# Modulation sums of ten of twelve blocks on ScalarE and GpSimd inside the attention loop, and a gated branch sum on VectorE instead of GpSimd

## The chip, the cores and the metric

The kernel runs on one core of a Trainium2 chip. The metric is the time of one execution on the device in microseconds (us), as the median of repeated runs. A profile of one execution is used beside it.

## What is computed

One layer of a hybrid backbone over 1024 latent tokens and 128 context tokens, with 1024 channels in float32. Of the reference this matters here:

```python
def modulation(cvec, w_ada, b_ada):
    m = jax.nn.silu(cvec) @ w_ada + b_ada
    return [t[:, None, :] for t in jnp.split(m, 6, axis=-1)]

def merge_branches(u_f, attn_o, g, w_fo, w_ao, w_out):
    gates = jax.nn.sigmoid(g)
    g_f, g_a = gates[..., :D_MODEL], gates[..., D_MODEL:]
    m = g_f * (fourier_mix(u_f) @ w_fo) + g_a * (attn_o @ w_ao)
    return m @ w_out
```

The layer is: modulated RMSNorm, one input projection that gives a Fourier branch, queries, keys and values (16 heads, 4 key heads, banded over blocks of 128 tokens) and two gate vectors; then the merge above, the output projection with a gated residual, and a squared-ReLU MLP with a gated residual. The modulation is two matrix-vector products (the conditioning vector and the context vector, called tokens 0 and 1) with a 1024 x 6144 matrix, w_ada. Its six parts are needed at different times: shift and scale of the first norm at once, the other four parts only from the output projection on.

## The kernel before, in words

All matrix products are done as three products of split operands: a float32 operand is cast to a reduced type ("hi", on ScalarE), the rest is taken by a subtraction ("lo", mostly on VectorE, helper `sub`, L138), and TensorE multiplies hi by hi, hi by lo and lo by hi (`mm3`, L191 to L193). Tokens lie in nine tiles of 128.

The program runs in stages. First the input is normalised and modulated, and the Fourier columns are projected. Then four Fourier groups are transformed (the loop over `gi`): per group a first product, an eviction to `pqh`/`pql` (L543 on ScalarE and L138 on VectorE), and a second product. Between them stand "filler" units, gate projections that TensorE can do at any time (`filler`; 48 units of 24 matmuls). Then keys and values are projected (`evac_kv`, with the rotary embedding `apply_rope`). Then comes attention: 36 units (4 key groups x 9 query tiles). The loop over units emits for unit s the queries of unit s+1, the scores of unit s (`attention_scores`, two pairs of heads), and the output of unit s-1 (`attention_out`). In `attention_scores` a pair of heads goes matmul (L691, L692), masked maximum (VectorE, L693), exponential (ScalarE, L705), reciprocal (VectorE, L713) and normalisation (GpSimd, L715). In `attention_out` the weights are transposed (TensorE, L729), split (ScalarE L734, VectorE L138) and multiplied with the values (L739, L740). Then come the Fourier output projections (`f_unit`), the attention output projection with the merge (8 column blocks x 3 token chunks, 24 turns, L905 to L914), the output projection, and the MLP.

The modulation of the four late parts is cut into 16 blocks of 256 columns, each block into ten steps (`mod_blocks`). Steps 0 to 7 load a 128 x 256 piece of w_ada (`mraw`, L296) and add its product with the two tokens to an accumulator `macc` (VectorE, L300 for the first piece, L302 for the others; two instructions per step). Steps 8 and 9 transpose and reduce the accumulator (VectorE, L311, L312). `mod_fold` (called at step 5 of the following block) sums over partitions by a matmul (TensorE, L265) and adds the bias (L269). `mod_step(n)` emits the next n steps. The constants place them: 30 steps (three blocks) in the Fourier loop (`MOD_F`), one step after each of units 1 to 30 (`MOD_A`), three steps in each merge turn (`MOD_2`) until 40 are left (`MOD_LATE`: 60 steps, six blocks), and the last four blocks in the MLP.

The order of instructions on an engine is not that of the text: a scheduler places each engine's instructions by its own model of times, `tc.issue_after(x)` keeps work from being placed before x, and from then on each engine and each queue works strictly in its order. SP issues almost all DMAs, in order too. The MLP's first piece is ordered by hand and is the same in both kernels.

```python
                for e in range(2):
                    nc.gpsimd.tensor_scalar(pt[:, e, :n], pt[:, e, :n], mx[:, 6 + e : 7 + e], 1.0, ALU.mult, ALU.mult)
                pts.append(pt)
...
                nc.vector.tensor_tensor(zf, zf, zp, ALU.mult)
                nc.gpsimd.tensor_tensor(z, z, zf, ALU.add)
```

## Time and profile before

| | |
|---|---|
| median of 3 runs | 1741.18 us (1739.69 to 1743.17) |
| the profiled execution | 1740.25 us |
| its span, first to last instruction | 1738.5 us |
| TensorE busy in the span | 1660.2 us, 95% |
| VectorE, ScalarE, GpSimd busy | 1217.1 us (70%), 846.3 us (49%), 229.2 us (13%) |
| mean granted TensorE clock | 0.982 |

In the profile PE is TensorE's matmuls, PEld its weight loads, DVE VectorE, ACT ScalarE, POOL GpSimd, and SP the queue that issues DMAs. Busy shares are averages over stages; the clock column is the granted clock as a part of full speed (1.2 GHz stands as 0.50, 2.4 GHz as 1.00).

### The profile page before, as it was taken

Reading aid. Unit: us, or ns where it says so; the run is one execution under the profiler, and the core shown is the slowest. Engines: PE = TensorE matmul, PEld = TensorE weight load, DVE = VectorE, ACT = ScalarE, POOL = GpSimd, SP = SyncE. Lnnn points to the kernel's source line nnn. Section 1 sums busy time; section 2 is a strip of 40 time slices with the busy share of each in tenths; the row PEclk is TensorE's granted clock in tenths of the full one; section 3 lists DMA queues with packets and bytes.
Section 4 is the critical chain, followed back from the end, with each engine's and each line's share of the span. In section 5 each row is a group of like instructions: output and inputs, shape, how many; then the busy total and the mean of one; then the engine's idle time right before and its main releaser. Section 6 shows DMA issues by size and latency. Waiting matters only on the chain.

```text
span 1738.5 us, 26472 instructions
## 1 busy us (share of the span) xinstructions
PE 1660.2 (95%) x9101; PEld 1480.9 (85%) x9101; DVE 1217.1 (70%) x2538; ACT 846.3 (49%) x1676; POOL 229.2 (13%) x310
## 2 busy tenths in 40 slices
PE   6999988999999999999899889999999999999998
PEld 5788878999899999999888688888888788888886
DVE  7595455686767777659968878767666488777764
ACT  7443134555646556655326663444444345444542
POOL 3410002212213222202211400000000100000000
PEclk9999999999999999999999989999999999999999
DMA  9462383032222211478655435444444997566751
GB/s 293 124 189 82 129 233 76 28 96 68 60 53 63 59 35 40 147 241 281 211 165 204 160 103 176 164 146 164 151 146 155 231 378 252 190 193 193 238 176 61
DMA packets 218759, 267.44 MB, mean 154 GB/s; under 512 B 30768, under 2 KB 150144, under 8 KB 218624
## 3 DMA queue, kind: packets, MB, share of 16 engines
q1 hardware_dynamic: 210368, 255.79, 46.3%
q0 software_dynamic: 8256, 9.96, 2.2%
q8 instruction: 72, 1.18, 0.3%
q14 instruction: 63, 0.52, 0.1%
HBM read 196.20 MB, written 69.48 MB: 153 GB/s over the span
## 4 chain that ended last, share of the span: by engine, by line
PE 43%; DVE 4%; DMA 2%; ACT 1%; issue 1%; POOL 0%; SPq 0%; ACTq 0%; DVEq 0%; POOLq 0%
PE x L1570 6%; PE x L1569 6%; PE x L1568 6%; PE x L1179 5%; PE x L1181 5%; PE x L1180 5%; PE x L1015 1%; PE x L1016 1%; PE x L1017 1%; DVE macc L302 1%; PE mm L1570 1%; PE mm L1569 1%; PE mm L1568 1%; PE mm L1226 1%; PE mm L1225 1%
## 5 line engine op out<-in xcount | busy, mean ns | idle before, releaser
L138 DVE TENSOR_TENSOR wlo<-wraw,whi 128x1024 fp32r<-128x1024 f32 x100 | 125.8, 1260 | 58.1 <-ACT whi L143 57.7
L143 ACT CAST whi<-wraw 128x1024 fp32r<-128x1024 f32 x98 | 102.5, 1049 | 88.8 <-DMA wraw<-in_w_ff_dram 21.0
L1569 PE MATMUL x<-BR 128*128 128x512 f32 x336 | 131.4, 391 | 0.0
L1570 PE MATMUL x<-BR 128*128 128x512 f32 x336 | 130.9, 391 | 0.0
L1568 PE MATMUL x<-BR 128*128 128x512 f32 x336 | 129.9, 391 | 0.0
L715 POOL TENSOR_SCALAR pt<-pt,mx 128x512 f32<-128x512 f32 (+2 forms) x144 | 99.1, 701 | 211.1 <-DVE mx L713 198.1
L705 ACT ACTIVATE pt<-pt,mx 128x513 f32<-128x513 f32 (+2 forms) x144 | 94.8, 661 | 55.8 <-DVE mx L703 55.1
L192 PE MATMUL mm<-BR,whi 128*128 128x384 f32 x336 | 113.8, 339 | 0.0
L693 DVE CUSTOM_DVE_ANT_0 pt<-s,mask,sink 128x512 f32<-128x512 f32 (+2 forms) x144 | 94.2, 673 | 22.2 <-PE ptp L729 15.0
L191 PE MATMUL mm<-BR,whi 128*128 128x384 f32 x304 | 105.3, 346 | 0.0
L193 PE MATMUL mm<-BR,wlo 128*128 128x384 f32 x304 | 102.9, 339 | 0.0
L1541 ACT CAST BR<-aa 128x512 fp32r<-128x512 f32 x80 | 49.7, 621 | 103.9 <-PE x L1569 49.1
L138 DVE TENSOR_TENSOR pl<-ptp,ph 128x512 fp32r<-128x512 f32 (+1 forms) x136 | 85.9, 640 | 15.6 <-ACT ph L734 14.5
L734 ACT CAST ph<-ptp 128x512 fp32r<-128x512 f32 (+1 forms) x136 | 72.7, 548 | 40.8 <-PE ptp L729 39.2
L302 DVE SCALAR_TENSOR_TENSOR macc<-mraw,siluc,macc 128x256 f32<-128x256 f32 x168 | 85.1, 544 | 10.5 <-DMA mraw<-in_w_ada_dram 10.3
L1179 PE MATMUL x<-BR,whi 128*128 128x512 f32 (+2 forms) x204 | 82.3, 403 | 6.2 <-ACT ZR L1203 3.3
L1181 PE MATMUL x<-BR,wlo 128*128 128x512 f32 (+2 forms) x204 | 81.1, 398 | 3.5 <-DVE wlo L138 3.5
L1180 PE MATMUL x<-BR,whi 128*128 128x512 f32 (+2 forms) x204 | 80.5, 395 | 0.0
L729 PE MATMUL ptp<-ident,pt 128*128 128x128 f32 x496 | 75.1, 273 | 3.0 <-ACT qT L675 3.0
L138 DVE TENSOR_TENSOR BR<-aa,BR 128x512 fp32r<-128x512 f32 x80 | 55.2, 689 | 32.0 <-ACT BR L1541 31.6
L1568 PEld LDWEIGHTS x<-BR 128*128 128x128 f32 x336 | 63.5, 189 | 13.2
L1569 PEld LDWEIGHTS x<-BR 128*128 128x128 f32 x336 | 63.4, 189 | 13.3
(422 smaller groups left out, 5119.6 us busy)
## 6 DMA issues: line engine op xcount, KB each, us to landing
aa<-hr_d SPq DMA_DIRECT2D x108, 256.0 KB, 3.4
ab<-in_w_ff_dram SPq DMA_DIRECT2D x108, 256.0 KB, 3.4
hr_d<-ZR SPq DMA_DIRECT2D x104, 256.0 KB, 4.1
wraw<-in_w_in_dram SPq DMA_DIRECT2D x40, 512.0 KB, 4.1
wraw<-in_w_ff_dram SPq DMA_DIRECT2D x34, 512.0 KB, 3.8
mraw<-in_w_ada_dram SPq DMA_DIRECT2D x96, 128.0 KB, 3.1
wraw<-in_w_out_dram SPq DMA_DIRECT2D x24, 512.0 KB, 3.8
z_d<-z SPq DMA_DIRECT2D x48, 192.0 KB, 1.9
```

The lines of the kernel that those rows point to most:

```text
L138: eng.tensor_tensor(dst, raw, hi.bitcast(F32), ALU.subtract)
L143: nc.scalar.copy(hi, raw)
L191: nc.tensor.matmul(out, ah, bh, start=start, stop=False)
L192: nc.tensor.matmul(out, ah, bl, start=False, stop=False)
L193: return nc.tensor.matmul(out, al, bh, start=False, stop=stop).ins
L302: nc.vector.scalar_tensor_tensor(acc[:, tok, :], wa, sc_, acc[:, tok, :], ALU.mult, ALU.add)
L1179: nc.tensor.matmul(po, wh, xh, start=(k == 0 and not cont), stop=False, skip_group_check=cont)
L1180: nc.tensor.matmul(po, wh, xl, start=False, stop=False, skip_group_check=cont)
L1181: nc.tensor.matmul(po, wl, xh, start=False, stop=(k == 3), skip_group_check=cont)
L1568: nc.tensor.matmul(ps, xh, bh, start=start, stop=False, skip_group_check=cont)
L1569: nc.tensor.matmul(ps, xh, bl, start=False, stop=False, skip_group_check=cont)
L1570: nc.tensor.matmul(ps, xl, bh, start=False, stop=stop, skip_group_check=cont)
```

## The change

The three blocks in the Fourier loop and four of the six blocks in the merge go to attention. There a block's steps 0 to 7 are done in another way: ScalarE multiplies the piece by the two tokens (`nc.scalar.activation` with a scale per partition, two instructions per step) into a single product buffer `mprod` (into `macc` for the first piece), and GpSimd adds the 128 x 512 product to `macc`. Steps 8 and 9 and the fold stay on VectorE and TensorE. Steps are emitted behind each pair's normalisation in `attention_scores`: two behind the first pair, one behind the second, until 60 are left, that is 100 steps, or ten blocks. Two blocks stay in the merge, on VectorE as before, now two steps per turn; four stay in the MLP. The sum of the two gated branches in the merge moves from GpSimd to VectorE. To make room, `apply_rope` writes its second product into its destination (`rb` falls away) and has one buffer `ra` instead of two.

```diff
-MOD_A = 1
-MOD_2 = 3
-MOD_F = (10, 10, 10, 0)
+MOD_A = (2, 1)
+MOD_2 = 2
+MOD_B = 60
...
-    MRB = [6, 2]
+    MRB = [2, 1]
+    split_mul = [True]
...
                         nc.sync.dma_start(wa, w_ada[k * P : (k + 1) * P, blk * MB : (blk + 1) * MB])
+                        if split_mul[0]:
+                            pr_ = acc if k == 0 else zpool[0].tile([P, 2, MB], F32, tag="mprod", name=nm("mprod"), bufs=1)
+                            for tok in range(2):
+                                nc.scalar.activation(pr_[:, tok, :], wa, AF.Copy, scale=siluc[:, tok, k : k + 1])
+                            if k:
+                                nc.gpsimd.tensor_tensor(acc, acc, pr_, ALU.add)
+                            return
...
             filler(FILL_F, anchor)
-            mod_step(MOD_F[gi])
...
-            a = p1.tile([P, 4, HD], F32, tag="ra", name=nm("ra"), bufs=2)
-            b = p1.tile([P, 4, HD], F32, tag="rb", name=nm("rb"), bufs=1)
+            a = p1.tile([P, 4, HD], F32, tag="ra", name=nm("ra"), bufs=1)
...
-            nc.vector.tensor_tensor(dst, a, b, ALU.add)
             if hi is not None:
-                nc.vector.tensor_tensor(hi, a, b, ALU.add)
+                nc.vector.tensor_tensor(hi, a, dst, ALU.add)
+            nc.vector.tensor_tensor(dst, a, dst, ALU.add)
...
-                    nc.gpsimd.tensor_scalar(pt[:, e, :n], pt[:, e, :n], mx[:, 6 + e : 7 + e], 1.0, ALU.mult, ALU.mult)
+                    ins = nc.gpsimd.tensor_scalar(
+                        pt[:, e, :n], pt[:, e, :n], mx[:, 6 + e : 7 + e], 1.0, ALU.mult, ALU.mult
+                    )
+                if len(msteps) > MOD_B:
+                    with tc.issue_after(ins.ins):
+                        mod_step(min(MOD_A[pr], len(msteps) - MOD_B))
...
-                if s <= 30:
-                    mod_step(MOD_A)
...
+        mod_step(len(msteps) - MOD_B)
+        mod_fold()
         f_unit(NF2)
...
-        MRB[:] = [4, 2]
+        MRB[:] = [4, 1]
+        split_mul[0] = False
...
-                nc.gpsimd.tensor_tensor(z, z, zf, ALU.add)
+                nc.vector.tensor_tensor(z, z, zf, ALU.add)
```

The change moves instructions in the scheduler's order at three places that the steps below speak of.

VectorE in the first Fourier group before; `pql` is the eviction behind which TensorE waits, `macc` the modulation sums, `wlo` the split of a weight:

```order
L138 TENSOR_TENSOR wlo_1708<-wraw_1705,whi_1707 128x1024
L302 SCALAR_TENSOR_TENSOR macc_1570<-mraw_1587,siluc,macc_1570 128x256
L138 TENSOR_TENSOR pql_1082<-x_1051,pqh_1081 128x512
L302 SCALAR_TENSOR_TENSOR macc_1570<-mraw_1597,siluc,macc_1570 128x256
L138 TENSOR_TENSOR stl_1239<-st_1228,sth_1238 128x1152
L138 TENSOR_TENSOR pql_1082<-x_1052,pqh_1081 128x256
L302 SCALAR_TENSOR_TENSOR macc_1570<-mraw_1597,siluc,macc_1570 128x256
L138 TENSOR_TENSOR pxl_1084<-x_1077,pxh_1083 128x256
```

and the same place with the change:

```order
L138 TENSOR_TENSOR wlo_1576<-wraw_1573,whi_1575 128x1024
L138 TENSOR_TENSOR pql_1082<-x_1051,pqh_1081 128x512
L138 TENSOR_TENSOR pql_1082<-x_1052,pqh_1081 128x256
L138 TENSOR_TENSOR stl_1199<-st_1188,sth_1198 128x1152
L138 TENSOR_TENSOR pxl_1084<-x_1077,pxh_1083 128x256
L138 TENSOR_TENSOR pql_1082<-x_1052,pqh_1081 128x128
```

The sums are gone from between the evictions.

GpSimd in attention with the change (before, only the rows of L687, here L692, and of L715, here L720, stand at this place); `pt` is a pair's weights, `mprod` a product of ScalarE:

```order
L692 COPY pt_2954<-sink_1648 128x2
L720 TENSOR_SCALAR pt_2954<-pt_2954,mx_2955 128x512 x2
L303 TENSOR_TENSOR macc_2784<-macc_2784,mprod_2973 128x512
L692 COPY pt_2983<-sink_1648 128x2
L303 TENSOR_TENSOR macc_2784<-macc_2784,mprod_2979 128x512
L720 TENSOR_SCALAR pt_2983<-pt_2983,mx_2984 128x512 x2
L303 TENSOR_TENSOR macc_2784<-macc_2784,mprod_3002 128x512
```

Three additions of 128 x 512 stand in a unit, one of them ahead of the second pair's normalisation.

ScalarE over the same unit with the change; the L301 rows are new:

```order
L301 ACTIVATE mprod_2973<-mraw_2971,siluc 128x256 x2
L710 ACTIVATE pt_2954,mx_2955<-pt_2954,mx_2955 128x513 x2
L744 CAST ph_2852<-ptp_2847 128x512
L753 COPY ot_2839<-o_2812 64x128
L754 COPY ot_2839<-o_2812 64x128
L744 CAST ph_2865<-ptp_2860 128x512
L680 COPY qT_2952<-ptp_2947 128x512
L301 ACTIVATE mprod_2979<-mraw_2977,siluc 128x256 x2
L710 ACTIVATE pt_2983,mx_2984<-pt_2983,mx_2984 128x513 x2
L301 ACTIVATE mprod_3002<-mraw_3000,siluc 128x256 x2
```

Each pair of products waits in ScalarE's queue for its piece of w_ada and for the addition before it, since there is one `mprod`. TensorE's fold matmuls go along: of the twelve folds ahead of the output projection, two stood in the Fourier loop, three in attention and seven from the merge's first turn on; with the change ten stand in attention and its tail, one behind the merge's eighth turn and one behind its last.

## Rows read from the trace of the kernel before

**Rows 1.** The page: busy time of each engine, its share, its instructions

```profile
PE 1660.2 (95%) x9101; PEld 1480.9 (85%) x9101; DVE 1217.1 (70%) x2538; ACT 846.3 (49%) x1676; POOL 229.2 (13%) x310
```

**Rows 2.** Stages: Fourier, keys and values, attention, merge (columns in the first row)

```profile
core 0: us, PE busy (x) PEld busy (x) DVE busy (x) ACT busy (x) POOL busy (x), PEclk, DMA share, GB/s
85.00:188.00 103.00, 98.17 (x529) 90.36 (x529) 68.45 (x152) 37.48 (x69) 10.04 (x8) 0.97 0.41 132
188.00:268.00 80.00, 72.01 (x337) 62.04 (x336) 41.76 (x86) 19.49 (x31) 3.11 (x6) 0.96 0.72 207
268.00:715.00 447.00, 432.04 (x3062) 417.87 (x3062) 322.46 (x921) 261.17 (x657) 112.17 (x209) 0.99 0.21 57
784.00:890.00 106.00, 97.97 (x530) 95.33 (x529) 97.97 (x208) 43.90 (x81) 29.90 (x24) 0.95 0.69 216
```

**Rows 3.** TensorE's waits, whole span: waiter, releaser, total us, times, longest us

```profile
PE mm L265 <- DVE red L312: 7.9, 4, 3.4
PE o L740 <- DVE pl L138: 5.3, 7, 1.4
PE x L191 <- ACT pqh L543: 4.5, 1, 4.5
...
PE ptp L729 <- ACT qT L675: 3.0, 2, 2.1
...
PE x L229 <- ACT whi L143: 2.5, 1, 2.5
PE ptp L670 <- DVE pl L138: 2.2, 3, 1.2
...
PE x L229 <- DVE rb L591: 1.7, 1, 1.7
```

**Rows 4.** Timeline, ScalarE: evictions of the first and third Fourier group (start, us)

```profile
123.37 0.63 ACT L543 CAST pqh<-x 128x512 fp32r<-128x512 f32 x1
...
132.64 0.39 ACT L543 CAST pqh<-x 128x128 fp32r<-128x128 f32 x1 [3.76 <-DVE pql L138]
...
156.92 0.63 ACT L543 CAST pqh<-x 128x512 fp32r<-128x512 f32 x1 [2.55 <-PE x L193]
...
161.88 0.41 ACT L543 CAST pqh<-x 128x128 fp32r<-128x128 f32 x1 [1.49 <-DVE pql L138]
```

**Rows 5.** Instructions on the modulation pieces: ns min/median/max, first and last start

```profile
L302 DVE SCALAR_TENSOR_TENSOR macc<-mraw,siluc,macc x168: 467/479/1517, 86.3 to 884.6; 128x256 f32<-128x256 f32 x168
...
L311 DVE STREAM_TRANSPOSE mraw<-macc x24: 396/432/442, 92.9 to 885.4; 128x256 f32<-128x256 f32 x24
L312 DVE TENSOR_REDUCE red<-mraw x24: 371/408/420, 93.6 to 886.0; 128x8 f32<-128x256 f32 x24
```

**Rows 6.** Groups in the merge, VectorE and GpSimd: busy us, mean ns, idle before

```profile
L908 DVE TENSOR_TENSOR z<-z,z 128x384 f32<-128x384 f32 x24 | 13.7, 571 | 4.2 <-DMA z<-part_d 2.8 <-ACT z L907 1.4
L909 POOL TENSOR_TENSOR z<-z,z 128x384 f32<-128x384 f32 x24 | 29.9, 1246 | 136.3 <-DMA mraw<-in_w_ada_dram 68.0 <-DVE z L905 42.6 <-issue 10.1
```

**Rows 7.** Nearest forms to the new work: ScalarE (min/median/max), GpSimd (busy, mean)

```profile
L1229 ACT ACTIVATE ZR<-ZR x16: 403/412/420, 1035.7 to 1376.7; 128x256 f32<-128x256 f32 x16
L1313 POOL TENSOR_TENSOR wraw<-wraw 128x512 f32<-128x512 f32 x1 | 1.6, 1615 | 0.1
```

**Rows 8.** The normalisation on GpSimd, and who waited for it (nobody)

```profile
L715 POOL TENSOR_SCALAR pt<-pt,mx x144: 371/692/1736, 281.9 to 723.1; 128x512 f32<-128x512 f32 x96, 128x384 f32<-128x384 f32 x32, 128x128 f32<-128x128 f32 x16
...
who waited for it (us, times):
busy tenths in 40 slices 0000002212212222200000000000000000000000
```

**Rows 9.** Groups of VectorE in attention with two SBUF inputs: busy, mean ns

```profile
L138 DVE TENSOR_TENSOR qhl<-qr,qhl 128x256 fp32r<-128x256 f32 x36 | 16.8, 467 | 0.5
L599 DVE TENSOR_TENSOR qhl<-ra,rb 128x256 fp32r<-128x256 f32 x32 | 14.2, 442 | 2.5 <-PE ptp L670 2.5
L597 DVE TENSOR_TENSOR qr<-ra,rb 128x256 f32<-128x256 f32 x32 | 13.5, 423 | 0.4
```

More of the change, by code (lines that the diff above doesn't have):

```diff
@@ L571, in backbone_kernel @@
         zpool[0] = p1
-        MRB[:] = [2, 1]
         identr = p1.tile([P, P], F32R, name="identr")
@@ L591, in apply_rope @@
             nc.vector.tensor_tensor(
-                b.rearrange("p h (d two) -> p h d two", two=2),
+                dst.rearrange("p h (d two) -> p h d two", two=2),
                 sw[:, :, :, ::-1],
@@ L622, in evac_kv @@
                     nc.sync.dma_start(out_k, kr)
-                    vo = p1.tile([P, NG, HD], F32, tag="ra", name=nm("ra"), bufs=2)
+                    vo = p1.tile([P, NG, HD], F32, tag="ra", name=nm("ra"), bufs=1)
                     nc.scalar.copy(vo, vps)
@@ L626, in evac_kv @@
                 nc.sync.dma_start(kr_d[:, t], kr)
-            vc = p1.tile([P, NG, HD], F32, tag="ra", name=nm("ra"), bufs=2)
+            vc = p1.tile([P, NG, HD], F32, tag="ra", name=nm("ra"), bufs=1)
             nc.sync.dma_start(vc, cache_v)
```

## The prediction

> **What bounds the kernel now.** The page comes first: TensorE is busy for 1660 of the 1738.5 us [rows 1]. The matmuls stay what they are, so the change can only win back time in which TensorE waits or runs at the lower clock, or add such time. The second view is the table by stages [rows 2], with the stages the change touches. In each, read the stage's length, TensorE's busy time and the granted clock. In the Fourier stage TensorE lacks 103.0 - 98.17 = 4.8 us; its clock of 0.97 costs about 0.03 x 103 = 3.1 us more, since the stretch at the lower level does that much less work: 7.9 us lost. For keys and values it is 8.0 + 3.2 = 11.2 us, for the merge 8.0 + 5.3 = 13.3 us. Attention lacks 15.0 us, with some 4 us of clock. The third view is TensorE's list of waits [rows 3], which says who ended the lost time. In the merge it is one kind: 7.9 us on the fold matmul, waiting for VectorE's reduction of a modulation block. VectorE is busy there for 97.97 of 106 us [rows 2], so the fold is late because its queue is full. In the Fourier stage one wait of 4.5 us stands for nearly all: TensorE waits for ScalarE's eviction `pqh`. The timeline [rows 4] shows why. In the first group the evictions take from 123.37 to 133.03 us, 9.7 us, and the last cast waits 3.76 us for VectorE's `pql`; in the third group, with no sums about, they take from 156.92 to 162.29 us, 5.4 us. In attention the waits are small and many, and VectorE ends more of them (5.3 and 2.2 us) than ScalarE (3.0 us).
>
> **The change part by part.**
>
> *Fourier loop.* Three blocks leave: 48 products of 0.479 us (the median, taken for all [rows 5]) and six transposes and reductions of 0.432 + 0.408 us, 28 us of VectorE time that stood ahead of and between the evictions, and 24 loads. If the first group's chain takes what the third's does, 9.7 - 5.4 = 4.3 us of the 4.5 go. In the new order the evictions stand side by side, but TensorE's second product is also placed some matmuls earlier, so I leave a wait of about 1 us: 4 us gained. With the wait goes most of the clock's fall behind it; I take 2 of 3.1 us. Sum: 6 us; bounds 0 (the chain then ends on a weight load) and 7.9.
>
> *Keys and values.* In the old order the scheduler had drawn attention's first steps forward to here; with the change each hangs behind a unit's normalisation. VectorE and the load queue lose them. Two waits can shrink, 2.5 us for a cast whose weight comes late and 1.7 us for the rotary embedding's last read of a bank [rows 3]; of these 4.2 us I take 2, bounds 0 and 4.2. The single buffer `ra` costs nothing: its writer and reader are both VectorE, in order, and only one load and one copy share it.
>
> *Merge.* Four blocks leave, each 16 x 0.479 + 2 x (0.432 + 0.408) = 9.3 us, together 37 us. The branch sum comes over from GpSimd: 24 additions, priced by the neighbour of the same shape at 0.571 us, 13.7 us [rows 6]. VectorE's demand falls by 23 of 98 us. Of the two blocks left, the first is drawn forward ahead of the merge, as VectorE has room there, so one fold stands inside the merge, with its reduction long done. I take 7.5 of 7.9 us and 4.5 of the 5.3 us of clock: 12 us; bounds 5 (half the waits stay, and the clock's half with them) and 13.3.
>
> VectorE shows a second thing here. The median of a product is 0.479 us and the longest 1.517 us [rows 5]: a product that starts while GpSimd adds waits that addition out, and GpSimd's additions take 1.246 us on the mean [rows 6]. With the sum on VectorE nothing is left to wait for in the merge; in attention the same is brought in, which the third rival prices.
>
> *Attention.* ScalarE gets ten blocks x 16 products. The nearest form, 128 x 256 from SBUF to SBUF, takes 0.412 us [rows 7]: 65.9 us, which lifts it from 261.2 to 327 of 447 us, 73%. GpSimd gets 70 additions of 128 x 512, nearest form 1.615 us [rows 7]: 113 us, from 112.2 to 225 us, 50%. VectorE gets twenty transposes and reductions, 16.8 us, from 322.5 to 339 us; the products before lay here only for a small part, which I count as nothing. GpSimd's work is covered: it does nothing else than normalise, and of the 144 normalisations none was waited for by anyone [rows 8], since a pair's weights are used one unit later. What stands behind a product in ScalarE's queue is not covered so well: `qT`, `ph` and the exponential. No row shows ScalarE at 73% in this stage, so I bound it. From below, nothing. From above, by VectorE, which at 322.5 of 447 us (72%) ends 7.5 us of TensorE's waits in two rows, against 3.0 us for ScalarE at 58%: as much as 4.5 us more at the same load, if it goes by load alone. I take that and 1.5 us for VectorE's added work: 6 us lost. That bound holds only as long as no product is itself held up; the second rival prices that. The 56 loads more find the DMA engines at a share of 0.21 [rows 2] and cost nothing; should one be late, it would be ScalarE's queue that stands, the same rival. The ten folds in attention wait for additions made a unit and more before; I add nothing for them.
>
> The output projection and the MLP keep their work; TensorE's order differs there at few places.
>
> **The sum.** -6 - 2 - 12 + 6 = -14 us. The profiled execution took 1740.25 us, 1.75 us more than its span and 0.9 us under the median of the runs shown, within their spread. 1740.25 - 14 = **1726 us**.
>
> **The rivals.**
>
> *All gaps close and attention pays nothing.* For it: GpSimd is idle for three quarters of attention, and ScalarE spends its time there waiting for others. Against it: a unit has three pairs of products more in ScalarE's ordered queue. Time: 1740.25 - 7.9 - 4.2 - 13.3 = 1715 us.
>
> *ScalarE's queue is held (slower).* There is one `mprod`, so a product waits for the addition before it, and that addition can stand behind a normalisation that waits for VectorE's reciprocal; `ph` and `qT` then wait behind the product. For it: the new order has three products per unit, two of them only one exponential apart. Against it: an addition takes 1.6 us and most products stand several instructions apart. Price: if each of 70 products is held for half an addition, 0.8 us, and TensorE feels half of it, 28 us. Time: 1740 - 20 + 28 = 1748 us. It decides from 20 / 70 = 0.29 us of TensorE time per product.
>
> *GpSimd's additions hold VectorE.* In attention the operations of VectorE with two SBUF inputs are the last three of the rotary embedding; the one that meets GpSimd most has a mean of 0.467 us against 0.423 us for the one that meets it least [rows 9], so it happens already with normalisations of 0.692 us. These 100 operations and some 16 splits of weights make 116. Additions cover 113 of 447 us, so 29 start inside one and lose half of 1.6 us each: 23 us of VectorE time. If all of it reaches TensorE: 1740 - 20 + 23 = 1743 us; my forecast has little of it there, since queries are made one unit ahead. The Trainium skill, "SBUF — State Buffer", section "Who interferes with whom", states this as a rule that speaks against the change: a VectorE operation with two SBUF inputs and a GpSimd operation that reads SBUF share a port, and the later one blocks until the first is done. The trace agrees, with the product of 1.517 us against 0.479; in full and unhidden the rule is this rival's 1743 us, while its other half, for the merge, is already in the 12 us.
>
> *The gaps stay.* The fold and the evictions might be ended by something else (a late weight load, a late `z`) once the sums are gone. Against it: the merge's waits all name VectorE's reduction. Half the gain: 1740.25 - 10 + 6 = 1736 us, or a little more.
>
> **How the numbers follow.** Forecast 0.52; all gaps close 0.17; ScalarE held 0.14; GpSimd holds VectorE 0.09; gaps stay 0.08. About 0.2%, 3.5 us, is what a measurement of this kernel can tell from no change. Faster by more than that are the forecast, the first rival and some of the last (0.03): 0.72. Within it: 0.09 + 0.05 = 0.14. Slower: 0.14. The range runs from 1713 us, the first rival with its 2 us of play, to 1744 us, which takes in the third; it leaves out part of the first rival and most of the second, under 2 in 10. The forecast's own range is 1719 to 1733 us.
>
> **What would show it.** Right: in the merge no wait of the fold for the reduction beyond 1 us in all, VectorE at about three quarters and the clock at 0.98 or more; in the Fourier stage the 4.5 us wait gone and the evictions of the first group done in 5 to 7 us; in attention ScalarE near 73%, GpSimd near 50%, TensorE's lost time up by some 6 us. Wrong: attention longer by 20 us and more, with TensorE's waits on `ph` or `qT` and ScalarE waiting for GpSimd (second rival) or the rotary embedding's operations well over 0.5 us on the mean (third); or a fold in attention that TensorE waits for; or a merge whose gaps only carry another name.

## The result, and the profile after

| | before | after |
|---|---|---|
| median of 4 runs each | 1741.35 us (1739.69 to 1743.17) | 1716.47 us (1713.90 to 1717.24) |
| ratio, 95% interval | | 0.985 (0.984 to 0.987) |
| the profiled execution's span | 1738.5 us | 1712.1 us |
| mean granted TensorE clock | 0.982 | 0.989 |

The change makes the kernel 24.9 us faster; 14 were forecast.

The page's line of busy times after it, beside [rows 1]:

```profile
PE 1649.8 (96%) x9101; PEld 1469.9 (86%) x9101; DVE 1178.2 (69%) x2402; ACT 909.4 (53%) x1836; POOL 285.9 (17%) x356
```

TensorE still has 9101 matmuls. VectorE's load falls by 39 us, ScalarE's rises by 63, GpSimd's by 57.

The table by stages, in the order of [rows 2] (Fourier, keys and values, attention, merge), each window at about the same place as before (the counts of TensorE's matmuls show that the work in it differs by up to 8%):

```profile
core 0: us, PE busy (x) PEld busy (x) DVE busy (x) ACT busy (x) POOL busy (x), PEclk, DMA share, GB/s
85.00:177.00 92.00, 92.00 (x516) 85.72 (x515) 44.74 (x84) 37.48 (x68) 8.41 (x8) 1.00 0.34 112
177.00:252.00 75.00, 72.30 (x360) 63.75 (x359) 28.08 (x49) 22.12 (x37) 2.70 (x6) 1.00 0.70 202
252.00:699.00 447.00, 429.70 (x3006) 410.04 (x3005) 346.10 (x948) 316.42 (x796) 199.32 (x276) 0.99 0.26 74
765.00:864.00 99.00, 99.00 (x572) 98.55 (x571) 71.76 (x144) 50.73 (x97) 0.00 (x0) 1.00 0.71 227
```

In three of the four, TensorE now runs at the full clock, and in two it has no gap that the table shows. VectorE in the merge is at 72% after 92%. In attention VectorE rises from 322 to 346 us, ScalarE from 261 to 316 and GpSimd from 112 to 199.

TensorE's longest waits after the change, whole span:

```profile
PE o L750 <- DVE pl L138: 5.1, 6, 1.7
PE x L1190 <- ACT ZR L1214: 4.8, 1, 4.8
PE s L696 <- DVE mx L698: 4.2, 8, 1.5
...
PE ptp L774 <- DMA kd<-kr_d: 2.7, 1, 2.7
...
PE q L191 <- DVE qr L596: 2.2, 4, 0.7
```

Against [rows 3], the wait of the fold (7.9 us) is gone, as are the one for `pqh` (4.5) and those for `whi` (2.5) and `rb` (1.7). New is the wait of attention's scores for VectorE, 4.2 us. The queries' wait for the rotary embedding's second product, 2.2 us, was there before, on `rb`, with 1.1 us.

The first Fourier group's evictions, timeline of ScalarE (start, us), beside [rows 4]:

```profile
121.59 1.13 ACT L551 CAST pqh<-x 128x512 fp32r<-128x512 f32 x2
124.10 0.41 ACT L551 CAST pqh<-x 128x128 fp32r<-128x128 f32 x1
126.01 0.42 ACT L551 CAST pqh<-x 128x128 fp32r<-128x128 f32 x1 [1.50 <-DVE pql L138]
```

They take 121.59 to 126.43 us, 4.8 us where it was 9.7.

For comparing many kernels one number per stage is handy. **TensorE's lost time** below is worked out from the matmul records: over all pairs of successive matmuls, the time from one start to the next, less the median of that time for matmuls of the same kind. It counts waits and low clock alike. Fourier begins at its first matmul on the transform, keys and values behind the last Fourier group, attention at the first transpose of keys and ends at its last output, the merge runs from there to the first matmul of the output projection. Times to the right are medians of the runs against the kernel before on the same chip (its medians there were 1740.4 to 1744.6 us). The columns of lost time come from one profile of each kernel, all set against the one profile of the kernel before, so a row's sum and its difference of medians can lie some us apart (e1b_gatedve: 9.0 us less in the spans, 14.3 in the medians). The level of attention's column hangs on what is counted as one kind; its step from before to after comes out between 8 and 9.5 us by other divisions too. The expectations of e1_gated and e5_dve give 27.8 and 31.5 us for attention without its tail; the column has the tail in it.

| kernel | Fourier | keys, values | attention | merge | output proj. | MLP | us, against before | ratio, 95% interval |
|---|---|---|---|---|---|---|---|---|
| before | 9.0 | 11.0 | 30.2 | 13.4 | 12.7 | 20.2 | | |
| **after** | 1.0 | 3.0 | 38.4 | 0.2 | 12.1 | 15.6 | -24.9 | 0.985 (0.984 to 0.987) |
| e1_gated | 8.3 | 11.1 | 33.6 | 12.6 | 12.7 | 17.5 | +2.3 | 1.002 (1.000 to 1.004) |
| e1b_gatedve | 7.7 | 3.0 | 30.3 | 13.6 | 12.4 | 20.6 | -14.3 | 0.992 (0.991 to 0.994) |
| e2_fourier | 8.2 | 3.1 | 43.3 | 0.5 | 12.9 | 15.9 | -9.8 | 0.995 (0.994 to 0.997) |
| e5_dve | 1.2 | 15.0 | 52.2 | 2.0 | 11.9 | 19.3 | +3.1 | 1.002 (1.001 to 1.003) |
| e5b_dvegated | 1.4 | 4.2 | 57.1 | 1.2 | 12.5 | 18.9 | -7.7 | 0.996 (0.995 to 0.998) |
| e9_all12 | 1.3 | 2.7 | 46.1 | 1.1 | 12.6 | 18.4 | -15.6 | 0.992 (0.989 to 0.995) |
| e11_eight | 1.3 | 2.6 | 37.2 | 0.8 | 11.8 | 21.3 | -26.6 | 0.985 (0.984 to 0.986) |
| e12_six | 1.1 | 4.0 | 36.7 | 2.5 | 16.2 | 18.9 | -20.7 | 0.987 (0.985 to 0.989) |
| e3_zpool | 1.5 | 2.8 | 38.7 | 0.4 | 21.4 | 21.5 | -16.8 | 0.990 (0.989 to 0.992) |
| e7_small | 1.0 | 2.9 | 47.0 | 0.3 | 12.3 | 20.6 | -18.2 | 0.990 (0.988 to 0.991) |
| e8_half | 1.0 | 3.3 | 36.5 | 1.0 | 12.3 | 18.2 | -27.6 | 0.985 (0.983 to 0.987) |
| e10_mix | 1.0 | 3.1 | 47.5 | 1.4 | 13.1 | 18.3 | -15.9 | 0.991 (0.989 to 0.993) |

Before to after, the stages give -8.0 - 8.0 + 8.2 - 13.2 - 0.6 - 4.6 = -26.2 us, against -26.4 in the spans. The MLP's column scatters between 15.6 and 21.5 us over kernels that do the same work in it, so its -4.6 is not put down to the change. The clock falls there at a few places in every run; why one run has more of them was not followed.

### The profile page after: what moved, and what is told of

It reads as the page before. It is cut to its first block, busy times and chain, and to the rows that moved or that the text cites. A ratio compares the mean times of both kernels' runs of the same rounds, so it can differ in the third digit from the quotient of the medians.

```text
span 1712.1 us, 26397 instructions
## 1 busy us (share of the span) xinstructions
PE 1649.8 (96%) x9101; PEld 1469.9 (86%) x9101; DVE 1178.2 (69%) x2402; ACT 909.4 (53%) x1836; POOL 285.9 (17%) x356
## 4 chain that ended last, share of the span: by engine, by line
PE 76%; DVE 8%; ACT 4%; DMA 3%; issue 2%; POOL 1%; SPq 0%; DVEq 0%; ACTq 0%; POOLq 0%
PE x L1580 6%; PE x L1579 6%; PE x L1581 6%; PE x L1190 6%; PE x L1192 6%; PE x L1191 6%; PE mm L191 3%; PE mm L192 3%; PE mm L193 3%; PE x L192 3%; PE x L193 3%; PE x L191 3%; PE ptp L739 2%; DVE pt L698 2%; PE o L750 1%
## 5 line engine op out<-in xcount | busy, mean ns | idle before, releaser
L138 DVE TENSOR_TENSOR wlo<-wraw,whi 128x1024 fp32r<-128x1024 f32 x100 | 123.7, 1239 | 85.0 <-ACT whi L143 84.7
L720 POOL TENSOR_SCALAR pt<-pt,mx 128x512 f32<-128x512 f32 (+2 forms) x144 | 97.5, 690 | 163.3 <-DVE mx L718 143.4
L138 DVE TENSOR_TENSOR pl<-ptp,ph 128x512 fp32r<-128x512 f32 (+1 forms) x136 | 86.1, 640 | 22.3 <-ACT ph L744 21.2
L303 POOL TENSOR_TENSOR macc<-macc,mprod 128x512 f32<-128x512 f32 x70 | 91.8, 1312 | 18.6 <-ACT mprod L301 18.4
L138 DVE TENSOR_TENSOR BR<-aa,BR 128x512 fp32r<-128x512 f32 x80 | 55.0, 687 | 31.7 <-ACT BR L1552 31.2
L301 ACT ACTIVATE mprod<-mraw,siluc 128x256 f32<-128x256 f32 x140 | 63.8, 502 | 20.5 <-POOL macc L303 20.0
L1579 PEld LDWEIGHTS x<-BR 128*128 128x128 f32 x336 | 63.1, 188 | 13.2
```

The source lines that it names most:

```text
L138: eng.tensor_tensor(dst, raw, hi.bitcast(F32), ALU.subtract)
L1579: nc.tensor.matmul(ps, xh, bh, start=start, stop=False, skip_group_check=cont)
```

## The experiments

### Keys and values: what stood there

*e1_gated*: the kernel before, attention's steps tied behind the normalisation.

```diff
-                    nc.gpsimd.tensor_scalar(pt[:, e, :n], pt[:, e, :n], mx[:, 6 + e : 7 + e], 1.0, ALU.mult, ALU.mult)
+                    ins = nc.gpsimd.tensor_scalar(
+                        pt[:, e, :n], pt[:, e, :n], mx[:, 6 + e : 7 + e], 1.0, ALU.mult, ALU.mult
+                    )
+                if pr == 1 and len(msteps) > 100:
+                    with tc.issue_after(ins.ins):
+                        mod_step(MOD_A)
...
-                if s <= 30:
-                    mod_step(MOD_A)
```

> The kernel before, with one thing changed: the thirty steps of the attention loop, still on VectorE, are tied behind the second pair's normalisation of their unit, so that the scheduler cannot draw them forward into the keys/values stage. Measured is TensorE's lost time by stage (a stage's length less its matmuls at their undisturbed pitch): before 9.0 us in the Fourier stage, 11.0 for keys and values, 27.8 in attention, 13.4 in the merge. Theory (the 8 us won for keys and values came from the steps that left that stage's VectorE and load queue): keys and values 11 to 3 or 4 us, the Fourier stage and the merge as before, attention up by 1 to 3 us, total 4 to 7 us under the kernel before, 1734 to 1737 us. Rival (the gain there came from the single buffer of the rotary embedding, or from the sums that left the Fourier loop just ahead of it): keys and values stay at 9 to 11 us, total within 3 us of the kernel before.

Keys and values still lost 11.1 us; attention's loss rose from 30.2 to 33.6, and the time by 2.3 us. The edit did not do what it says. In the new order 32 products stand ahead of attention as before: a tie to a GpSimd instruction holds only what GpSimd itself does, and these steps are VectorE's. This run tells nothing of either theory. In the changed kernel the same tie works, most likely because a step's addition is on GpSimd and the single `mprod` holds back ScalarE's products behind it: in its trace four products stand ahead of attention, two into the first `macc` and two into the first `mprod`, and the other 156 in it.

*e1b_gatedve*: the same, tied to the reciprocal on VectorE.

```diff
-                nc.vector.reciprocal(mx[:, 6:8], mx[:, 4:6])
+                rin = nc.vector.reciprocal(mx[:, 6:8], mx[:, 4:6])
...
+                if pr == 1 and len(msteps) > 100:
+                    with tc.issue_after(rin.ins):
+                        mod_step(MOD_A)
```

> The kernel before, with the thirty steps of the attention loop tied behind the reciprocal of the second pair on VectorE itself. (Tying them behind the normalisation on GpSimd, tried first, left the 32 products between the rotary embedding's instructions: the tie holds only work of the engine that it names. In this kernel's order none is left there and 48 stand in attention.) Theory (what stood in the keys/values stage made it lose 8 us): keys and values 11 to 3 or 4 us, Fourier 8 to 9 and merge 12 to 14 as before, attention up by 2 to 4 us for 32 products more: 1734 to 1738 us against 1740 to 1741. Rival (the gain there came from the sums that left the Fourier loop, or from the rotary embedding's single buffer): keys and values 9 to 11 us, the time as before or up by the 2 to 4 us.

14.3 us faster (9.0 in the spans), where 2 to 7 were expected, and the stage's loss falls to the 3.0 us of the changed kernel. The table by stages, keys and values of this kernel, and TensorE's only wait listed in it:

```profile
179.00:256.00 77.00, 74.29 (x366) 65.62 (x365) 28.19 (x49) 20.12 (x33) 2.69 (x6) 1.00 0.68 194
```

```profile
PE ptp L767 <- DMA kd<-kr_d: 2.7, 1, 2.7
```

VectorE's 42 us of [rows 2] are 28, the clock is whole, and the waits for `whi` and `rb` are gone. The 8 us are the two blocks' 32 products and their 16 loads, taken together; which of the two weighs more was not tried. Since all else is the kernel before, neither the single `ra` nor the Fourier loop has a part in it. Attention took the 32 products at no loss: 30.3 against 30.2 us.

### The Fourier loop: three blocks put back

*e2_fourier*:

```diff
-    MRB = [2, 1]
-    split_mul = [True]
+    MRB = [6, 2]
+    split_mul = [False]
...
             filler(FILL_F, anchor)
+            mod_step((10, 10, 10, 0)[gi])
...
+        MRB[:] = [2, 1]
+        split_mul[0] = True
```

> The changed kernel, with the thirty steps of the Fourier loop put back there on VectorE; seven blocks stay in attention on ScalarE and GpSimd. Theory (the sums in front of the evictions made the Fourier stage lose 8 us): the Fourier stage loses 7 to 9 us again instead of 1.0, attention loses 2 to 3 us less since three blocks of ten are gone from it, keys and values stay at 3: 4 to 7 us slower than the changed kernel, 1720 to 1723 us. Rival (the Fourier gap closed because TensorE's second product was placed elsewhere, or goes into another stage): the same as the changed kernel within 2 us, or the loss moves to keys and values.

The Fourier stage loses 8.2 us again, and TensorE's list of waits has the old row back:

```profile
PE x L191 <- ACT pqh L551: 4.6, 1, 4.6
```

Keys and values stay at 3.1, so the two stages' losses are separate. The surprise is attention: with seven blocks instead of ten it loses 43.3 us, 4.9 more. In all it is 15 us slower than the changed kernel by the table's differences, where 4 to 7 were expected.

### The engines in attention

*e5_dve*: the ten blocks' steps on VectorE (`split_mul = [False]`).

> The changed kernel, with the ten blocks of attention worked on VectorE as the others are, at the same places: no products on ScalarE, no additions on GpSimd. VectorE gets 160 products of 0.479 us, 77 us, on its 346 us of 447 (which fall by some 25 us, as nothing holds it any more): about 398 us, 89%. Theory (it is the engine load in attention that costs, and the split is worth something): attention loses 8 to 15 us more than the 31.5 us of the changed kernel, total 1722 to 1730 us. Rival (the split buys nothing; what counts is only that the sums left the other stages): within 3 us of the changed kernel.

3.1 us slower than the kernel before. The tie being to GpSimd, 48 products went forward into the keys/values stage (15.0 us lost), and attention lost 52.2.

*e5b_dvegated*: the same, tied to the reciprocal on VectorE (`with tc.issue_after(rin.ins)`).

> The changed kernel with the ten blocks on VectorE, as in the run with all products on VectorE, but each step tied behind its pair's reciprocal on VectorE, so that all 160 products stand in attention and none in the keys/values stage, where 48 of them cost 12 us before (15.0 against 3.0 us lost). Theory 1 (the division among engines matters in attention itself): keys and values back at 3 us, attention and its tail lose 50 to 60 us against 38.4 in the changed kernel: 1730 to 1740 us. Theory 2 (the place is all that matters; VectorE could have carried the products): attention and its tail within 5 us of 38.4, 1713 to 1722 us.

Keys and values recover (4.2), attention loses 57.1 us. Its stage:

```profile
252.00:699.00 447.00, 416.35 (x2895) 396.78 (x2895) 373.96 (x1058) 241.32 (x604) 120.25 (x194) 0.98 0.25 71
```

VectorE is at 84%, TensorE fits 111 matmuls fewer into the same 447 us than in the changed kernel. So VectorE carried three blocks in attention for nothing (e1b_gatedve), but not ten: the two kernels lie 57.1 - 38.4 = 18.7 us of lost time apart. Not all of it need be the division among the engines, since the tie and the order differ as well, and kernels with ScalarE and GpSimd at work lose between 36.5 and 47.5 us at six to twelve blocks. What lies above them all is 9.6 us.

*e7_small*: GpSimd's addition cut short.

```diff
-                                nc.gpsimd.tensor_tensor(acc, acc, pr_, ALU.add)
+                                nc.gpsimd.tensor_tensor(acc[:, :, :4], acc[:, :, :4], pr_[:, :, :4], ALU.add)
```

> The changed kernel with the addition on GpSimd cut from 128x512 to 128x8 (4 of 256 columns per token): 70 additions stay at their places and release ScalarE as before, but take some 0.2 us instead of 1.31 us. The rest of the sum of products is left out. Theory (GpSimd's additions hold VectorE for some 20 us, and ScalarE for 20 us, but TensorE feels little of it): attention and its tail lose 30 to 36 us instead of 38.4, total 1706 to 1712 us. Rival A (the additions are what attention pays): loss down to the 30 us of the kernel before or less, total 1704 us or less. Rival B (all of it is hidden, the 8 us are ScalarE's own products): 38 us, 1714 to 1717 us. VectorE's busy time in attention falls by 15 to 25 us in all three.

Groups in attention, the changed kernel first, then this one (busy us, mean ns):

```profile
L303 POOL TENSOR_TENSOR macc<-macc,mprod 128x512 f32<-128x512 f32 x70 | 91.8, 1312 | 18.6 <-ACT mprod L301 18.4
...
L604 DVE TENSOR_TENSOR qr<-ra,qr 128x256 f32<-128x256 f32 x32 | 22.1, 689 | 0.6
...
L603 DVE TENSOR_TENSOR qhl<-ra,qr 128x256 fp32r<-128x256 f32 x32 | 19.4, 608 | 4.5 <-PE ptp L675 4.4
```

```profile
L303 POOL TENSOR_TENSOR macc<-macc,mprod 128x8 f32<-128x8 f32 x70 | 17.1, 244 | 20.5 <-ACT mprod L301 20.5
L604 DVE TENSOR_TENSOR qr<-ra,qr 128x256 f32<-128x256 f32 x32 | 14.2, 445 | 0.4
L603 DVE TENSOR_TENSOR qhl<-ra,qr 128x256 fp32r<-128x256 f32 x32 | 13.5, 423 | 1.0 <-PE ptp L675 0.9
```

The hold is real: the rotary embedding's operations go back from 689 and 608 ns to 445 and 423. VectorE's busy time in the whole stage falls from 367.0 us in 491 to 345.9 in 501. And yet attention loses 47.0 us, 8.6 more. All three theories fail. The scheduler, seeing shorter additions, wrote another order on every engine, and that order costs 8.6 us more than the short additions save. What the additions alone cost TensorE therefore stays open.

*e8_half*: one buffer per token, two half additions.

```diff
-                            pr_ = acc if k == 0 else zpool[0].tile([P, 2, MB], F32, tag="mprod", name=nm("mprod"), bufs=1)
                             for tok in range(2):
-                                nc.scalar.activation(pr_[:, tok, :], wa, AF.Copy, scale=siluc[:, tok, k : k + 1])
-                            if k:
-                                nc.gpsimd.tensor_tensor(acc, acc, pr_, ALU.add)
+                                ac = acc[:, tok, :]
+                                pr_ = ac if k == 0 else zpool[0].tile([P, MB], F32, tag="mprod", name=nm("mprod"), bufs=2)
+                                nc.scalar.activation(pr_, wa, AF.Copy, scale=siluc[:, tok, k : k + 1])
+                                if k:
+                                    nc.gpsimd.tensor_tensor(ac, ac, pr_, ALU.add)
```

> The changed kernel with one product buffer per token, two of 128x256 in the space of the one of 128x512, and two additions of 128x256 on GpSimd instead of one of 128x512. A product then waits for the half addition before the last, not for the whole one just before it. Theory (ScalarE's 20 us of waits for additions reach TensorE in part): ScalarE's wait for GpSimd falls to under 8 us, attention and its tail lose 2 to 5 us less, total 1711 to 1715 us. Rival (ScalarE has the room; the half additions cost GpSimd a start-up each and hold VectorE more often): same or up to 4 us slower, 1716 to 1720 us.

ScalarE's wait for the additions, changed kernel first:

```profile
ACT mprod L301 <- POOL macc L303: 20.0, 23, 2.0
```

```profile
ACT mprod L302 <- POOL macc L304: 14.6, 29, 1.5
```

It falls, by less than expected; attention's loss is 36.5 and the ratio the same 0.985. The order differs widely again, so this is no clean test either, but nothing in it speaks for a price of ScalarE's hold.

*e10_mix*: token 0's product on VectorE, token 1's on ScalarE and GpSimd.

```diff
+                                if k and tok == 0:
+                                    nc.vector.scalar_tensor_tensor(ac, wa, sc_, ac, ALU.mult, ALU.add)
+                                    continue
```

> The changed kernel with a step's work shared by three engines: token 0's product on VectorE as before (70 products of 0.48 us), token 1's on ScalarE (80 of 0.5 us) with a 128x256 addition on GpSimd (70 of some 0.75 us, in two buffers). Thirty steps carried by VectorE alone cost attention nothing when tied behind the reciprocal (30.3 us lost against 30.2 before). Theory (attention pays for the additions that hold VectorE and ScalarE, and VectorE has room for about three blocks' worth): attention and its tail lose 30 to 35 us instead of 38.4, total 1708 to 1713 us. Rival (the scheduler's order, which any such edit changes, moves the loss more than the load does: runs with seven and twelve blocks lost 43 and 46 us): anything from 36 to 46 us, total 1714 to 1725 us.

Attention loses 47.5 us. The rival holds, even past its upper end: in this order, relieving GpSimd and ScalarE bought nothing.

### How many blocks go where

*e9_all12*: twelve blocks in attention, none in the merge.

```diff
-MOD_A = (2, 1)
+MOD_A = (2, 2)
...
-MOD_B = 60
+MOD_B = 40
```

> The changed kernel, with the two blocks of the merge in attention too, four steps per unit instead of three, so that none is left in the merge. Theory (the merge has nothing left to lose, 0.2 us, and each step in attention costs by its load): attention and its tail lose 2 to 4 us more, total 1716 to 1719 us. Rival (VectorE's remaining sums in the merge delay the output projection, which still loses 12 us): output projection down by 2 us or more and total 1710 to 1713 us. Second rival (a fourth step per unit tips ScalarE's queue over): attention loses 10 us more, 1725 us.

Attention loses 46.1 us, 7.7 more, and nothing is won behind it (12.6 in the output projection). Nearest is the second rival; whether ScalarE's queue or the new order did it, this run doesn't tell.

*e11_eight*: eight blocks, four left to the merge.

```diff
-MOD_B = 60
+MOD_B = 80
```

> The changed kernel with eight blocks in attention instead of ten, and four on VectorE from the merge's stage on instead of two. Theory 1 (load sets attention's loss, VectorE's load the merge's): attention and its tail lose 36 to 37 us instead of 38.4; the merge, which lost 13.4 with six blocks and the sum on GpSimd and 0.2 with two, loses 3 to 7 us: total 1717 to 1722 us. Theory 2 (order sets attention's loss, within 36 to 46 us whatever the number of blocks): attention outside 34 to 38 us, and the merge by itself as in theory 1. If the merge loses under 1 us with four blocks, two of the four that left it bought nothing.

As fast as ten blocks, within the intervals. Attention lost 37.2, near theory 1. The merge with four blocks on VectorE lost only 0.8, so two of the four that left it bought nothing.

*e12_six*: six blocks, and six in the merge.

```diff
-MOD_2 = 2
+MOD_2 = 3
...
-MOD_B = 60
+MOD_B = 100
```

> The changed kernel with six blocks in attention instead of ten and six in the merge, as many as before, three steps per turn, with the branch sum on VectorE. With four blocks there the merge lost 0.8 us; the same two blocks with the sum on GpSimd cost 9 us in the output projection. VectorE's load in the merge is the one of before, 98 us of 106, plus 13 us for the sums, so it is over-full by this count. Theory 1 (VectorE's demand decides): the merge loses 10 us or more, total 1726 us or more. Theory 2 (the hand-over to GpSimd and back was the merge's trouble, not the blocks): the merge and the output projection lose 0 to 3 us more than the changed kernel's 12.3 together, total 1712 to 1720 us, with attention and its tail at 34 to 38 us; that version would be the equal of the changed kernel or better.

It comes out between the theories: 18.7 us lost in merge and output projection, 6.4 more than in the changed kernel. But the merge itself, with the sum on VectorE, loses 2.5 us where it lost 13.4. It is not quite the same work: the scheduler put the last block's 16 products and two of the six folds behind the first matmul of the output projection, so 80 products stand in the merge where 93 stood before. Its row by stages and the fold's wait:

```profile
765.00:864.00 99.00, 97.45 (x561) 96.34 (x560) 91.01 (x211) 49.14 (x93) 0.00 (x0) 1.00 0.80 256
```

```profile
PE mm L266 <- DVE red L320: 1.5, 1, 1.5
```

VectorE is as full as before, 92% in both, and still the fold waits 1.5 us and not 7.9, with the clock at 1.00. The output projection behind it loses 16.2 instead of 12.1 us; its waits for a weight's cast (`whi`) grow from 1.1 to 3.3 us and the one for `ZR` behind it from 4.8 to 7.1. The products in the merge, before and here (busy us, mean ns):

```profile
L302 DVE SCALAR_TENSOR_TENSOR macc<-mraw,siluc,macc 128x256 f32<-128x256 f32 x70 | 39.1, 587 | 0.9 <-DMA mraw<-in_w_ada_dram 0.8
```

```profile
L310 DVE SCALAR_TENSOR_TENSOR macc<-mraw,siluc,macc 128x256 f32<-128x256 f32 x84 | 38.0, 478 | 1.4 <-DMA mraw<-in_w_ada_dram 1.3
```

With the additions gone from GpSimd a product takes 109 ns less.

### The branch sum

*e3_zpool*: the changed kernel with the sum on GpSimd.

```diff
-                nc.vector.tensor_tensor(z, z, zf, ALU.add)
+                nc.gpsimd.tensor_tensor(z, z, zf, ALU.add)
```

> The changed kernel with the sum of the two gated branches back on GpSimd; TensorE's order is the same row for row as in the changed kernel, so only the place of the sum differs. Theory (the four blocks that left the merge are what emptied VectorE there; the sum's place matters little): the merge loses 0 to 2 us instead of 0.2, total 1716 to 1719 us. Rival (the sum's place is part of the gain: GpSimd's 24 additions of 1.25 us hold VectorE's products and the other z operations, and the output projection gets its operands later): the merge loses 4 us or more, total 1720 us or more.

TensorE's order is untouched here, so this is the cleanest pair of all (the order of VectorE and ScalarE shifts in some rows), and attention's loss reproduces (38.7 against 38.4). The rival is right, though at another place than the merge: its loss is 0.4, and the output projection's goes from 12.1 to 21.4. The timeline at its start, TensorE, then GpSimd and ScalarE:

```profile
867.38 0.50 PE L1026 MATMUL x<-whi,BR 128*128 128x512 f32 x1 [2.62 <-DVE z L916]
...
870.13 0.80 PE L1026 MATMUL x<-whi,BR 128*128 128x512 f32 x1 [1.79 <-DVE z L916]
```

```profile
863.87 1.85 POOL L920 TENSOR_TENSOR z<-z,z 128x384 f32<-128x384 f32 x1 [2.61 <-DVE z L916]
...
867.46 1.02 POOL L920 TENSOR_TENSOR z<-z,z 128x384 f32<-128x384 f32 x1 [1.74 <-issue]
```

```profile
868.51 0.51 ACT L924 CAST BR<-z 128x384 fp32r<-128x384 f32 x1 [2.24 <-POOL z L920]
```

This is the path of a merge result: multiplication (VectorE, L916), sum (GpSimd, L920), cast (ScalarE, L924), split (VectorE, L138). The two matmuls do not wait for a late result at its end. The row names L916: it reads a merge product out of a bank `x`, one of six, and the output projection's first matmuls write `x` again, so they wait until L916 has emptied the bank. VectorE works in order, and a turn's split stands ahead of the next turn's multiplication (L916), so the steps form a loop over three engines. Its turn is the distance from one L916 to the next. VectorE's rows, this kernel, then the changed one at the same place:

```profile
863.19 0.55 DVE L916 TENSOR_TENSOR z<-x,z 128x384 f32<-128x384 f32 x1
863.66 1.22 DVE L138 TENSOR_TENSOR wlo<-wraw,whi 128x1024 fp32r<-128x1024 f32 x1
866.30 0.56 DVE L138 TENSOR_TENSOR BT<-z,BT 128x384 fp32r<-128x384 f32 x1 [1.43 <-ACT BT L924]
866.77 0.55 DVE L916 TENSOR_TENSOR z<-x,z 128x384 f32<-128x384 f32 x1
869.05 0.56 DVE L138 TENSOR_TENSOR BR<-z,BR 128x384 fp32r<-128x384 f32 x1 [1.73 <-ACT BR L924]
869.53 0.55 DVE L916 TENSOR_TENSOR z<-x,z 128x384 f32<-128x384 f32 x1
871.79 0.56 DVE L138 TENSOR_TENSOR BR<-z,BR 128x384 fp32r<-128x384 f32 x1 [1.72 <-ACT BR L924]
872.27 0.55 DVE L916 TENSOR_TENSOR z<-x,z 128x384 f32<-128x384 f32 x1
```

```profile
862.33 0.55 DVE L916 TENSOR_TENSOR z<-x,z 128x384 f32<-128x384 f32 x1
862.91 0.56 DVE L920 TENSOR_TENSOR z<-z,z 128x384 f32<-128x384 f32 x1
864.05 0.56 DVE L138 TENSOR_TENSOR BR<-z,BR 128x384 fp32r<-128x384 f32 x1 [0.58 <-ACT BR L924]
864.53 0.55 DVE L916 TENSOR_TENSOR z<-x,z 128x384 f32<-128x384 f32 x1
```

The last turns take 3.58, 2.76 and 2.74 us against 2.20. The longest has the addition of 1.85 us in it, which ran beside VectorE's split of a weight. So the multiplications of 866.77 and 869.53 us come late, the matmuls of 867.38 and 870.13 us start as they end, and the output projection waits 4.4 us. The clock falls behind these waits, by the table of windows:

```profile
870.00:876.00 6.00, 5.87 (x14) 4.67 (x15) 3.87 (x11) 2.31 (x4) 2.00 (x2) 0.50 0.01 3
877.00:883.00 6.00, 6.00 (x28) 4.96 (x27) 2.19 (x2) 1.06 (x1) 0.00 (x0) 1.00 0.98 344
```

14 matmuls in six microseconds at 0.50 (1.2 GHz), 28 in six at 1.00 (2.4 GHz) behind them. GpSimd's additions also hold the 28 products that are left in the merge, 478 ns each in the changed kernel:

```profile
L310 DVE SCALAR_TENSOR_TENSOR macc<-mraw,siluc,macc 128x256 f32<-128x256 f32 x28 | 15.3, 588 | 2.1 <-DMA mraw<-in_w_ada_dram 2.1
```

Merge and output projection together now stand as a square: 26.1 us before; 21.8 with four blocks gone and the sum on GpSimd; 18.7 with all six blocks and the sum on VectorE; 12.3 with both. The sum's place is worth 7.4 to 9.5 us, the four blocks 4.3 to 6.4, and of the latter nearly all comes with the first two (12.6 at four left). TensorE's order is the same only in the pair with two blocks left, 9.5 us apart by lost time and 8.1 by the medians; the other two corners differ in their order and in earlier stages as well.

## Why the prediction was right, and where its sizes were not

Its direction, its places and its range held: 1716 us lies between 1713 and 1744, though 10 us under the point and outside the forecast's own 1719 to 1733. That it came inside the range is in part luck: the lower end was set by the rival in which attention pays nothing, and attention paid 8.2 us. Keys and values, with 6.0 us more than forecast, and the MLP, with 4.6 us that the change does not explain, made up for it. Term by term:

- **Fourier, -6 forecast, -8.0 found.** The step is right: the wait for `pqh` went, the group's evictions take 4.8 us, and putting the blocks back brings 7.2 us of loss and the same row back. What was held back for a wait of 1 us and for part of the clock was not needed.
- **Keys and values, -2 forecast, -8.0 found.** This is the step that failed most. "of these 4.2 us I take 2, bounds 0 and 4.2" left out of the bound the clock, which the prediction itself had priced at 3.2 us, and took half of the waits. e1b_gatedve shows that both waits and the whole fall of the clock hung on 32 products and 16 loads.
- **Merge, -12 forecast, -13.2 found there, -13.8 with the output projection.** The size is right, the account of it is not. It said that "VectorE's demand falls by 23 of 98 us", and booked the branch sum as 13.7 us of added cost. By the square, the sum's move is the larger half of the gain, and in e12_six VectorE at the same 92% loses 2.5 us instead of 13.4, or 18.7 instead of 26.1 with the output projection. That GpSimd's additions hold a VectorE product was seen ("the longest 1.517 us") but given no price; that product in fact stood in the Fourier stage (121.49 us), beside another addition, and the longest in the merge took 1.244 us. The rows give the price: 70 products of the merge at 587 ns and not 478 are 7.6 us of VectorE time. Nor is the lower bound of 5 us what it is said to be, for half of 13.3 is 6.65.
- **Attention, +6 forecast, +8.2 found.** The size is right; that load makes it is only partly shown. From six to eight to ten blocks the loss goes 36.7, 37.2, 38.4 us, 1.7 us for 40 steps. If that is the load's doing and holds for the first sixty steps too, ten blocks cost some 4 us by load, but orders alone move the loss by more. TensorE's named waits in attention rise only from 14.8 to 17.8 us, with the clock at 0.99 in both; the rest is in short delays between matmuls that no row names. ScalarE is at 71% (73 forecast), GpSimd at 45% (50), and prices were off both ways: a product took 502 ns, not 412, an addition 1312, not 1615.
- **MLP, 0 forecast, -4.6 found**, within the scatter of that column.

**The rivals.** *All gaps close and attention pays nothing* comes nearest in time, 1715 us, but is wrong in its second half: attention pays 8, and the missing gain comes from keys and values (8.0 against 4.2) and the MLP. *ScalarE's queue is held*: 20.0 us of holding were there, in 23 waits, at 2.0 us the longest. It was priced at 56 us (70 products, 0.8 us each). *GpSimd's additions hold VectorE*: the hold came to 21 us by e7_small (all of VectorE's work) against 23 priced, and its sign, the rotary embedding's operations well over 0.5 us, is there, but the time is not, since 8.2 us is all that attention lost, whatever its causes. The row that shows it, beside [rows 9], is the one of `qr<-ra,qr`, 689 ns against 423. The Trainium skill, "SBUF — State Buffer", section "Who interferes with whom", says that an instruction of VectorE with two SBUF inputs and a reading one of GpSimd shut each other out for a whole instruction; the trace agrees in the row above. *The gaps stay* is out: three stages run at 1.00.

Not settled: which places in the order make attention lose 37 us in some kernels and 43 to 47 in others. Seven blocks lost more than ten, short additions more than long ones, so the number of steps and the load do not explain it alone. In three of the four with 43 to 47 TensorE's query transposes wait most for VectorE's `pl` (5.8 to 11.4 us in all, 2.0 in the changed kernel), but e8_half, at 36.5, has 5.5 us of the same. With eight blocks, or with two half buffers, the kernel is as fast as the changed one; none was faster beyond the intervals.

## What to carry to other kernels

A small operation on GpSimd between two steps of VectorE can cost TensorE time though GpSimd is nearly idle: here it lengthened the loop in which the next tile's work stands behind this one's, held VectorE's two-input work meanwhile, and was held by it. Ask for its place before its engine's load. Work without a due time should be tied to the engine that does it; a scheduler draws it forward into the stage that can least bear it, and here 32 products with their loads cost 8 us in the wrong stage and none in the right one. When TensorE waits for an engine, price the clock that falls behind the wait along with the wait itself.

## What the runs showed of the hardware

A tiny VectorE operation with one SBUF input is held too. The scaling of two maxima, 128 x 2, in attention of the changed kernel:

```profile
L708 DVE TENSOR_SCALAR mx<-mx x72: 124/161/1241, 260.9 to 715.0; 128x2 f32<-128x2 f32 x72
```

Its median is 161 ns, the longest 1241; before, with normalisations alone on GpSimd, the longest was 436. The one of 1241 ns ran from 366.36 to 367.60 us, beside an addition on GpSimd from 366.28 to 367.58. ScalarE's exponential waits for this operation. The Trainium skill, "SBUF — State Buffer", section "Who interferes with whom", lists this form among those that can take the shared ports; the row agrees.

An addition of 128 x 512 in float32 on GpSimd took 1271 to 1532 ns. In e3_zpool one of 128 x 384 took 1.0 us in most turns and 1.85 us where it ran beside a weight split of 1.22 us.
